# First half's attention by pairs of heads, block by block inside the second half's pairs

## The chip, the cores and the metric

The kernel runs on one core of one Trainium2 chip. The metric is the device time of one execution in microseconds (us); a run's time is compared as the median of several executions. The profile records one execution of its own. Its engines are PE (TensorE, matrix products; PEld is its weight load), DVE (VectorE), ACT (ScalarE), POOL (GpSimd) and SP (the queue that issues the DMAs).

## The reference

One layer of a streaming encoder: a norm with conditioning, one input projection, two groups of heads (an RWKV-7 recurrence and a forgetting attention, eight heads of 64 each), one output projection onto the concatenation of both, a gated residual, and a feed-forward part with a second gated residual. 1024 frames are a new stream, 64 are the next frames of another stream that has 256 cached frames. The change touches only the attention of the 1024 frames and what stands beside it:

```python
def _fox_attend(q, k, v, lc_q, lc_k, pos_q, pos_k):
    s = jnp.einsum('bqhd,bshd->bhqs', q, k, preferred_element_type=jnp.float32) * (HEAD_DIM ** -0.5)
    decay_bias = jnp.transpose(lc_q, (0, 2, 1))[..., :, None] - jnp.transpose(lc_k, (0, 2, 1))[..., None, :]
    causal = pos_k[None, :] <= pos_q[:, None]
    p = jax.nn.softmax(jnp.where(causal, s + decay_bias, -jnp.inf), axis=-1)
    return jnp.einsum('bhqs,bshd->bqhd', p.astype(v.dtype), v)
...
    mix = jnp.concatenate([y_rwkv, y_fox], axis=-1) @ w_out
    x = x + gt1[:, None] * mix
```

## The kernel before

**Halves.** The frames are worked in two halves, `Half(0)` with frames 0 to 511 and `Half(1)` with frames 512 to 1023 and the 64 frames of the other stream (576 columns). `phase` (from line 1595) runs the input projection and the recurrence for one half after the other, in an order written out by hand (`ORDER`). Keys and queries go to DRAM (`kx`, `qx`) in a high and a low part, since a float32 product is made of three products of parts; values go there by tokens (`vtok`), and for the first half also split into parts, by `put_v` (line 849), into `vscr`. What remains of the recurrence after the second half's projection (`late`, line 1758) is one head pair's norm.

**The first half's attention** (`attend`, line 927) goes head by head. Each head has two units of 256 queries. A unit makes the scores of its queries (two products and a causal mask each, line 956 to 962), takes the row maximum on VectorE, the exponential with the row sum on ScalarE, scales, transposes the result on the tensor engine, splits it into two parts, and multiplies both with the split values. `Pipe(2)` keeps two units in flight besides the one that is started. The heads' outputs go to DRAM (`yscr`). Heads 0 to 2 run while the recurrence's memory is still held, heads 3 to 7 after it. Beside heads 5 to 7 the operands and the row maxima of the second half's first pair are made (lines 1787 to 1791).

**The second half's attention** (`att_second`, line 1244) goes by pairs of heads, four of them. Operands come in by `pair_load` (line 1045) in three parts: 0 for the maxima, 1 for the scores, 2 for the values. `att_max` (line 1071) makes scores only to take row maxima; `att_rows` (line 1097) puts the negated maxima into a row of an operand, so that the scores come out shifted. `att_main` (line 1109) then makes the scores with the keys on the partitions, block by block of 128 keys, takes the exponential straight from PSUM, adds the blocks up for the denominators (`total`; VectorE for one head, GpSimd for the other), multiplies with the values, float32 without a split (`values`), and at the end makes the denominators with a product by ones. No transposition of the scores is needed. `att_main` stops ("h", "b", the block's number, "v") so that `att_second` can put other work between: the maxima of the next pair, and the output projection of the first half (`proj_steps`, line 1225), 64 steps of three products, as its operands arrive by `load_mix` (line 1284) from `yscr` and is split. In this stretch `te.on` is set: the tensor engine's instructions keep the order of the program. Elsewhere a scheduler orders each engine's instructions.

**Memory.** A pool of tiles that is opened where others were closed waits tile by tile until what lay there is no longer used. The second half's operands (`pair_ops`, line 1024) lie where the recurrence's tiles were. PSUM has eight banks; the second half's attention uses three for scores (`st`), two for maxima and small results (`mx`), two for the projection (`mm`), one for the values (`pv`).

**After it** come the second half's output projection (`outproj`), the feed-forward part (`ffn`) and its second product (`down`), which the change leaves as they are.

Of the kernel before, what the change touches and what calls it, by code (L numbers as in the profile page):

```python
# [64 lines left out]
class K:  # L65
# [782 lines left out]

    def put_v(self, j, src, b0, nb, rows):

        nc = self.nc
        s = src.rearrange("p i (h d) -> p i h d", h=2)
        for h in range(2):
            vs = self.slot([P, 4, 2, 64], F32R, name="vs", tag="fx")
            d = vs[0:rows, 0:nb]
            nc.vector.tensor_copy(d[:, :, 0], s[:, :, h])
            nc.vector.tensor_tensor(d[:, :, 1], s[:, :, h], d[:, :, 0].bitcast(F32), op=ALU.subtract)
            nc.sync.dma_start(self.vscr[2 * j + h][0:rows, b0:b0 + nb], d.rearrange("p i x d -> p i (x d)").bitcast(F32))
# [24 lines left out]
    def att_consts(self, ap):  # L883
# [11 lines left out]
        self.nmx = [ap.tile([P, 64], F32, name=f"nmx{x}") for x in range(2)]  # L895
# [3 lines left out]
    def att_pools(self, es, R):  # L899
        nc = self.nc  # L900
        self.tpool = MultiPool({t: R(es, "t" + t, b) for t, b in (("pth", 3), ("ptl", 3), ("nm", 4), ("ls", 4))})
        self.spool.pools.update({"fy": R(es, "sfy", 2), "avt": R(es, "savt", 2)})

    def att_ops(self, p, sets):

        return [[p.tile(s, F32R, name=f"{n}x{i}") for n, s in (("qs", [P, 512]), ("q2", [68, 512]), ("k1", [P, 512]),
                                                                  ("k2", [68, 512]), ("vs", [P, 4, P]))] for i in sets]

    def att_load(self, hd, hf):
        nc = self.nc  # L910
        qs, q2, k1, k2, vs = self.ops[hd > 1][hd % 2]
        n, t0 = hf.n, hf.t0
        NK = SP + PAST + SS if hf.smp else 512
        nc.sync.dma_start(qs[:, 0:n].bitcast(F32), self.qx[hd, 0:128, t0:t0 + n])
        for r in (0, 64):
            nc.sync.dma_start(k1[r:r + 64, 0:NK].bitcast(F32), self.kx[hd, 0:64, 0:NK])
        for r in (slice(0, 64), slice(64, 68)):
            s = slice(64 + r.start, 64 + r.stop)
            nc.sync.dma_start(q2[r, 0:n].bitcast(F32), self.qx[hd, s, t0:t0 + n])
            nc.sync.dma_start(k2[r, 0:NK].bitcast(F32), self.kx[hd, s, 0:NK])  # L920
        if hf.smp:
            nc.sync.dma_start(vs[:, 0:10].bitcast(F32), self.vscr[hd][:, 0:10])
            nc.sync.dma_start(vs[0:SS, 10].bitcast(F32), self.vscr[hd][0:SS, 10])
        else:
            nc.sync.dma_start(vs[:, 0:4].bitcast(F32), self.vscr[hd][:, 0:4])

    def attend(self, hd, hf):

        nc = self.nc
        j, h = hd // 2, hd % 2  # L930
        hs = slice(64 * h, 64 * h + 64)
        qs, q2, k1, k2, vs = self.ops[hd > 1][hd % 2]
        n, t0 = hf.n, hf.t0
        if hd > 1:
            self.att_load(hd, hf)
        if h == 0:
            self.fy = self.slot([P, n], name="fy", tag="fy")
        fy = self.fy
        qps = list(range(2, 5) if hf.smp else range(2))

        def unit(qp):
            smp = qp == 4
            nq = SS if smp else 256
            kb = 3 if smp else 2 * qp + 2
            pTs = []
            ptiles = []
            for t in range(1 if smp else 2):
                q0 = SP if smp else (2 * qp + t) * P
                nk = 320 if smp else q0 + P
                k0 = SP if smp else 0  # L950
                qn = SS if smp else P
                pq = self.ps([P, 1024 if hf.smp else 512], tag="sc", name="psc")
                c = 0
                while c < nk:
                    w = 320 if smp else min(512, -(-(nk - c) // 256) * 256)
                    nc.tensor.matmul(pq[:, c:c + w], qs[:, q0 - t0:q0 - t0 + P], k1[:, k0 + c:k0 + c + w], start=True,
                                     stop=False, skip_group_check=True)
                    nc.tensor.matmul(pq[:, c:c + w], q2[0:68, q0 - t0:q0 - t0 + P], k2[0:68, k0 + c:k0 + c + w], start=False,
                                     stop=False, skip_group_check=True)
                    c += w  # L960
                cm = 0 if smp else nk - qn
                nc.tensor.matmul(pq[0:qn, cm:cm + qn], self.identb[0:qn, 0:qn], self.cmask[0][0:qn, 0:qn], start=False,
                                 stop=True, skip_group_check=True)
                nm = self.tpool.tile([P, 1], F32, tag="nm", name="nm")
                ls = self.tpool.tile([P, 1], F32, tag="ls", name="ls")
                nc.vector.tensor_reduce(nm[0:qn], pq[0:qn, 0:nk], axis=AX.X, op=ALU.max, negate=True)
                p = self.tpool.tile([P, 1024 if hf.smp else 512], F32, tag="p", name="p")
                nc.scalar.activation(p[0:qn, 0:nk], pq[0:qn, 0:nk], AF.Exp, bias=nm[0:qn], accum_out=ls[0:qn])
                nc.vector.reciprocal(ls[0:qn], ls[0:qn])
                self.flip = (self.flip + 1) % 3  # L970
                if self.flip == 0:
                    nc.scalar.activation(p[0:qn, 0:nk], p[0:qn, 0:nk], AF.Copy, scale=ls[0:qn])
                else:
                    nc.vector.tensor_scalar(p[0:qn, 0:nk], p[0:qn, 0:nk], ls[0:qn], None, op0=ALU.mult)
                ptiles.append((p, qn, nk))
            yield 1
            for b0 in range(0, kb, 2):
                pt = self.ps([P, 2, 256], tag="tr", name="ppt")
                pT = [self.tpool.tile([P, 2, 256], F32R, tag=t, name=t) for t in ("pth", "ptl")]
                pTs.append(pT)  # L980
                for b in range(b0, min(kb, b0 + 2)):
# [10 lines left out]
                elif not smp and b0 + 2 == kb:  # L992
                    for t in pT:
                        nc.gpsimd.memset(t[:, 1, 0:P].bitcast(F32), 0.0)
# [249 lines left out]
    def att_second(self, hf, h0, g):  # L1244
# [6 lines left out]
        for j in range(4):  # L1251
# [26 lines left out]
            if j == 2:  # L1278
                mix = self.load_mix(hf)
# [769 lines left out]
```

## Time and profile before

| | us |
|---|---|
| median of three runs | 1715.62 |
| lowest and highest run | 1715.6 and 1720.08 |
| profiled execution | 1710.58 |
| its span, first to last instruction | 1708.9 |
| PE busy | 1634.3 (96%) |
| DVE busy | 1073.4 (63%) |
| ACT busy | 686.0 (40%) |
| POOL busy | 163.7 (10%) |

The page divides the span into 40 slices of 42.7 us and gives each engine's busy share in tenths. The tensor engine stands at 9 nearly everywhere and at 7 in the 17th and 18th slices, from 684 to 769 us, which is most of the first half's attention. The granted clock (PEclk) is at 5 in the 18th slice and at 8 in the 19th. A matrix product's duration contains its way through the array; products follow each other closer than that, so the price of one is read from start to start. A product at half clock counts as busy all the time it takes.

### The profile page before, as it was taken

The numbers are of one execution on the slowest core, as the hardware profiler recorded it, in microseconds if no ns is written. First come the engines' busy times: TensorE is split into PE (matmuls) and PEld (weight loads), VectorE is DVE, ScalarE is ACT, GpSimd is POOL, SyncE is SP. The second block draws the span as 40 slices with busy tenths as digits, with TensorE's granted clock in tenths as the row PEclk, the third lists the DMA queues.
The fourth block names the chain that finished last, engine by engine and source line by source line (L and its number), as shares of the span: only waits on it lengthen the run. The fifth ranks groups of instructions, "written<-read, shape, count | busy, mean of one in ns | idle before, by whom it ended". The sixth has DMA issues, their size and how long they took to land.

```text
span 1708.9 us, 32239 instructions
## 1 busy us (share of the span) xinstructions
PE 1634.3 (96%) x12811; PEld 1409.5 (82%) x12811; DVE 1073.4 (63%) x2264; ACT 686.0 (40%) x1374; POOL 163.7 (10%) x312
## 2 busy tenths in 40 slices
PE   5999999999999999779999999999999999999999
PEld 3667667788878887555668999999999999999998
DVE  6676675758866644756556995555555555555545
ACT  4544465654445445624335652322332233211210
POOL 1101101020201103202341000000000000000000
PEclk9999999999989999958999999999999999999999
DMA  8434376621233253645634423222222214433313
GB/s 315 154 109 138 105 211 193 191 70 50 54 90 89 77 147 116 195 130 146 170 125 144 165 100 104 82 80 79 81 80 80 77 64 158 148 100 96 96 38 124
DMA packets 131909, 203.81 MB, mean 119 GB/s; under 512 B 61966, under 2 KB 68654, under 8 KB 131758
## 3 DMA queue, kind: packets, MB, share of 16 engines
q1 hardware_dynamic: 131758, 201.75, 38.6%
q8 instruction: 101, 1.65, 0.4%
q14 instruction: 50, 0.41, 0.1%
HBM read 155.62 MB, written 46.07 MB: 118 GB/s over the span
## 4 chain that ended last, share of the span: by engine, by line
PE 49%; DMA 2%; DVE 1%; ACT 1%; SPq 1%; issue 1%; DVEq 0%
PE pd L1582 15%; PE pfe L1467 8%; PE pfc L1467 7%; PE pfa L1467 7%; PE pfb L1467 4%; PE po L1929 2%; PE pst L1929 2%; PE pav L1929 1%; DMA kax<-kx 1%; PE pmx L1929 1%; PE po L325 1%; PE po L323 1%; PE po L324 1%; SPq L1049 1%; DMA kbx<-kx 0%
## 5 line engine op out<-in xcount | busy, mean ns | idle before, releaser
L323 PE MATMUL pmm<-hhi,whi 128*128 128x288 f32 (+1 forms) x624 | 221.2, 355 | 4.0 <-ACT pb L346 4.0
L324 PE MATMUL pmm<-hlo,whi 128*128 128x288 f32 (+1 forms) x624 | 217.8, 349 | 0.9 <-DVE hlo L301 0.7
L325 PE MATMUL pmm<-hhi,wlo 128*128 128x288 f32 (+1 forms) x624 | 215.5, 345 | 0.0
L241 ACT CAST whi<-wraw 128x1024 fp32r<-128x1024 f32 (+2 forms) x116 | 99.3, 856 | 216.8 <-PE pd L1582 165.0
L1582 PE MATMUL pd<-al,whi 128*128 128x512 f32 (+1 forms) x528 | 172.4, 327 | 0.0
L1582 PE MATMUL pd<-ah,whi 128*128 128x512 f32 (+1 forms) x528 | 172.2, 326 | 0.0
L1582 PE MATMUL pd<-ah,wlo 128*128 128x512 f32 (+1 forms) x528 | 172.2, 326 | 0.0
L1586 DVE SCALAR_TENSOR_TENSOR x1t<-pd,mod,x1t 128x512 f32<-128x512 f32 x192 | 91.2, 498 | 109.1 <-PE pd L1582 108.5
L323 PEld LDWEIGHTS pmm<-hhi,whi 128*128 128x128 f32 x624 | 120.2, 193 | 19.3 <-ACT pb L346 5.8
L324 PEld LDWEIGHTS pmm<-hlo,whi 128*128 128x128 f32 x624 | 120.3, 193 | 12.8 <-issue 2.1
L325 PEld LDWEIGHTS pmm<-hhi,wlo 128*128 128x128 f32 x624 | 119.9, 192 | 11.6 <-issue 2.2
L245 DVE TENSOR_TENSOR wlo<-wraw,whi 128x1024 fp32r<-128x1024 f32 (+2 forms) x108 | 104.2, 965 | 31.0 <-ACT whi L241 30.6
L1582 PEld LDWEIGHTS pd<-ah,whi 128*128 128x128 f32 x528 | 99.0, 188 | 7.1
L1582 PEld LDWEIGHTS pd<-ah,wlo 128*128 128x128 f32 x528 | 99.1, 188 | 7.1
L1582 PEld LDWEIGHTS pd<-al,whi 128*128 128x128 f32 x528 | 99.1, 188 | 7.0
L1467 PE MATMUL pfc<-hh,hS 128*128 128x256 f32 (+1 forms) x352 | 101.8, 289 | 1.1 <-ACT hh L1369 1.1
L1467 PE MATMUL pfa<-hh,whi 128*128 128x256 f32 (+1 forms) x352 | 102.1, 290 | 0.0
L1467 PE MATMUL pfc<-hh,lS 128*128 128x256 f32 (+1 forms) x352 | 101.8, 289 | 0.0
L1467 PE MATMUL pfa<-hl,whi 128*128 128x256 f32 (+1 forms) x352 | 101.7, 289 | 0.0
L1467 PE MATMUL pfa<-hh,wlo 128*128 128x256 f32 (+1 forms) x352 | 101.5, 289 | 0.0
L1467 PE MATMUL pfc<-hl,hS 128*128 128x256 f32 (+1 forms) x352 | 100.7, 286 | 0.0
L1414 ACT CAST hS<-wraw 128x512 fp32r<-128x512 f32 x88 | 53.6, 619 | 62.7 <-PE pfc L1467 61.5
(421 smaller groups left out, 4160.2 us busy)
## 6 DMA issues: line engine op xcount, KB each, us to landing
wraw<-in_w_in_dram SPq DMA_DIRECT2D x52, 512.0 KB
wada<-in_w_ada_dram SPq DMA_DIRECT2D x48, 512.0 KB
as<-actscr SPq DMA_DIRECT2D x22, 544.0 KB
wraw<-in_w_gate_dram SPq DMA_DIRECT2D x22, 512.0 KB
wraw<-in_w_up_dram SPq DMA_DIRECT2D x22, 512.0 KB
wraw<-in_w_down_dram SPq DMA_DIRECT2D x40, 256.0 KB
wraw<-in_w_out_dram SPq DMA_DIRECT2D x16, 512.0 KB
actscr<-sg SPq DMA_DIRECT2D x22, 288.0 KB
```

Of the source, the lines that this page charges most:

```text
L241: nc.scalar.copy(hi, src)
L245: eng.tensor_tensor(lo, src, hi.bitcast(F32), op=ALU.subtract)
L323: nc.tensor.matmul(ps[0:M, 0:n], whi[:, k, 0:M], xhi[:, k, off:off + n], start=(k == 0), stop=False)
L324: nc.tensor.matmul(ps[0:M, 0:n], whi[:, k, 0:M], xlo[:, k, off:off + n], start=False, stop=False)
L325: nc.tensor.matmul(ps[0:M, 0:n], wlo[:, k, 0:M], xhi[:, k, off:off + n], start=False, stop=(k == kt - 1))
L1049: ld = lambda d, s: nc.sync.dma_start(d.bitcast(F32), s)
L1414: nc.scalar.copy(w[x][0], src)
L1467: nc.tensor.matmul(ps, l[:, k], r[:, s, k], start=(first and k == 0 and y == 0), stop=(k == 3 and y == 2), skip_group_check=True)
L1582: nc.tensor.matmul(ps[:, 0:n], w[:, i], x[:, t:t + n], start=(i == 0 and y == 0), stop=(i == len(fs) - 1 and y == 2))
L1586: nc.vector.scalar_tensor_tensor(dst, ps[:, so - off:so - off + l], self.mod[:, 40 + o, b:b + 1], dst, op0=ALU.mult, op1=ALU.add)
L1929: return self.pin(self.tc.nc.tensor.matmul(*a, **k))
```

## The change

The first half's attention goes by pairs as well. Pair 0 runs alone, beside the rest of the recurrence, with operands of its own (`pair_first`). Pairs 1 to 3 run inside the second half's pairs: `low_steps` makes a generator of 39 steps, and `att_second` takes one of them at each stop of the second half's own generator, 25 stops a pair, before any other filler. The operands of pairs 1 to 3 are tiles that lie idle then: the mixes of both halves (`mixhi`, `mixlo`), of which pair 3 takes over those of pair 1; their exponentials and sums lie in the tile of the residual (`x1`). So the residual's loads and the loads of the mixes start when pair 3 is done, and the output projection two blocks later, now three steps a block. Outputs of pairs 1 to 3 are split into the mixes at once; only pair 0's goes by `yscr`, and `load_mix` brings five parts in place of eight. `attend`, `att_load`, `att_ops`, `att_pools`, `put_v` and `Pipe` go. The PSUM pools of the attention are opened ahead of pair 0, and the tiles of `pair_ops` lie in another order. While `te.on` is set, `total` gives the second head's adds to GpSimd in either half. There are four tiles of maxima in place of two.

```diff
-        else:
-            self.put_v(j, vt, 0, 4, P)
...
+    def pair_first(self, pool):
+
+        g = {n: [pool.tile([r, 512], F32R, name=f"{n}f{h}") for h in range(2)]
+             for n, r in (("kb", 73), ("qc", 73), ("ka", P), ("qa", P), ("qb", 73))}
+        for h in range(2):
+            self.ones_keys(g["kb"][h])
+            self.no_rows(g["qc"][h])
+        return self.pair_bufs(g, True)
+
+    def pairs_low(self):
+
+        (m0, m1), (l0, l1) = self.mixhi, self.mixlo
+        a, b, c, d, e, f = [[t[:, k, 0:512] for k in range(4)] for t in (m0.a, l0.a, m1.a, l1.a, m0.b, l0.b)]
+        one = {"kb": a[0:2], "qc": a[2:4], "ka": b[0:2], "qa": b[2:4], "qb": c[0:2]}
+        two = {"kb": c[2:4], "qc": d[0:2], "ka": d[2:4], "qa": [e[2], f[2]], "qb": [e[3], f[3]]}
+        out = [None, one, two, dict(one)]
+        x, n = self.x1[0], [0]
+
+        def pt():
+            n[0] += 1
+            return x[:, n[0] % 6]
...
+            free = iter((6, 7))
+            g["pt"], g["acc"] = pt, lambda free=free: x[:, next(free)]
+            self.pair_bufs(g, False)
+        return out
...
-                eng = nc.gpsimd if h and hf.smp else nc.vector
+                eng = nc.gpsimd if h and te.on else nc.vector
...
-        if hf.smp:
+        if hf.smp or j:
             self.split(self.mixhi[hf.i][:, 4 + j, 0:n], self.mixlo[hf.i][:, 4 + j, 0:n], fy[:, 0:n])
...
+    def low_steps(self, hf, gs):
+
+        fill = lambda it, n: [next(it, None) for _ in range(n)]
+        for j in (1, 2, 3):
+            mx = self.att_max(j + 1, hf, gs[j + 1]) if j < 3 else iter(())
+            last = 0
+            for b in self.att_main(j, hf, gs[j]):
+                if b in ("h", "b"):
+                    fill(mx, 2 * (last > 1))
+                elif b == "v":
+                    if j == 1:
+                        for x in range(3):
+                            self.pair_load(3, hf, gs[3], x)
+                    fill(mx, 99)
+                    if j < 3:
+                        self.att_rows(j + 1, hf, gs[j + 1])
+                else:
+                    last = b + 1
+                yield
...
             for b in self.att_main(j, hf, g):
+                if low and next(low, 1) == 1:
+                    low, mix = None, self.load_mix(h0)
+                    fill(mix, 2)
+                    self.residual_x(h0)
+                    start = 8 * j + (b if isinstance(b, int) else 7) + 2
...
-                    fill(po, self.MIX[b])
+                    if start and 8 * j + b == start:
+                        po = self.proj_steps(h0)
+                    fill(po, 3)
                     fill(mx, b % 2)
-                if b == 2 and j == 0:
-                    self.residual_x(h0)
...
+            for _ in self.att_main(0, halves[0], self.g0):
+                pass
             at0.close()
             mid.close()
...
+            self.pair_load(1, halves[0], gs[1], 0)
+            for x in range(3):
+                self.pair_load(0, halves[1], g, x)
+                if x:
+                    self.pair_load(1, halves[0], gs[1], x)
+            for j, hf, q in ((1, halves[0], gs[1]), (0, halves[1], g)):
+                for _ in self.att_max(j, hf, q):
+                    pass
+                self.att_rows(j, hf, q)
...
+            self.att_second(halves[1], halves[0], g, self.low_steps(halves[0], gs))
```

More of the change, by code (lines that the diff above doesn't have):

```diff
@@ L1030, in pair_ops, with pair_bufs @@
         for t in self.pops["kb"]:
-            self.nc.gpsimd.tensor_copy(t[64:69], self.ones[64:69, 0:1].to_broadcast([5, nk]))
+            self.ones_keys(t)
         for t in self.pops["qc"]:
-            self.nc.gpsimd.memset(t[64:69].bitcast(F32), 0.0)
+            self.no_rows(t)
             self.nc.gpsimd.memset(t[:, 576:640].bitcast(F32), 0.0)
+    def pair_bufs(self, g, big):
+        for n, m in (("pt", 512), ("acc", 512), ("r", 512), ("fy", 576)):
+            if n not in g:
+                g[n] = lambda n=n, m=m: self.tpool.tile([P, m], F32, tag=n, name=n)
+        g["tags"] = {"st": "st", "mx": "mx", "pv": "pv" if big else "mm", "sm": "mx"}
+        return g
@@ L1064, in pair_load @@
                 ld(ka[:, 0:NK], self.kx[hd, 0:128, 0:NK])
-        if part == 2:
+        if part == 2 and not hf.smp:
+            g["v"] = self.tpool.tile([P, 4, P], F32, tag="v0", name="v0")
+            nc.sync.dma_start(g["v"], self.vtok[j][:, 0:4])
+        elif part == 2:
             v = g["v"]
@@ L1287, in load_mix @@
         mh, ml = self.mixhi[hf.i], self.mixlo[hf.i]
-        for m in range(4 if hf.smp else KT):
+        for m in range(4 if hf.smp else 5):
             t = self.slot(name="mixt", tag="fs")
@@ L1780, in run @@
+            p = L(mix1, "mix1")
+            high = [rows4(p, halves[1], x) for x in ("mixrh", "mixfh", "mixrl", "mixfl")]
             self.x1 = [L(x1s, "x1p0").tile([P, KT, 512], F32, name="x1_0")]
-            self.tpool.pools["pc"] = L(attp, "tpc", 2)
             self.pair_ops(L(attp, "attp"))
-            g = self.pair_get(0)
-            mx = self.att_max(0, halves[1], g | {"tags": {"mx": "ch"}})
-            for hd in range(3, 8):
-                pipe.run(self.attend(hd, halves[0]))
-                if hd > 4:
-                    self.pair_load(0, halves[1], g, hd - 5)
-                for _ in range(16 * (hd > 5)):
-                    with tc.issue_after(self.av.ins):
-                        next(mx, None)
@@ L1801, in run @@
-            self.mixlo = [Rows(rows4(p, hf, "mixrl"), rows4(p, hf, "mixfl")) for p, hf in zip(mps, halves)]
-            self.spool.pools.update({"fs": L(mix0, "sfs", 2)})
-            self.tpool.pools.update({t: R(att, "t" + t, b) for t, b in (("pt", 6), ("acc", 2), ("r", 1), ("fy", 1), ("pts", 1),
-                                                                        ("accs", 1))})
-            PB = lambda es, name, b: E(es, name, b, space=PSUM, reuse_waits="tile")
-            self.pspool = MultiPool({t: PB(att, "p" + t, b) for t, b in (("st", 3), ("pv", 1), ("mm", 2), ("mx", 2))})
```

233 lines of the change are left out of this document (51 added, 182 removed).

## The prediction

> **What bounds the kernel now.** I read the windows view first, because the change touches one stretch only: from the end of the projections (671 us) to the start of the second half's output projection. Its columns are the stretch, its length, the busy time of each engine, then the granted TensorE clock and the DMA share and rate.
>
> ```profile
> span 1708.9 us, 32239 instructions
> ...
> core 0: us, PE busy (x) PEld busy (x) DVE busy (x) ACT busy (x) POOL busy (x), PEclk, DMA share, GB/s
> 671.00:693.00 22.00, 16.81 (x103) 12.46 (x101) 18.08 (x49) 16.09 (x46) 5.26 (x15) 1.00 0.64 199
> 693.00:728.00 35.00, 25.55 (x137) 19.09 (x138) 24.49 (x72) 21.40 (x66) 8.68 (x24) 0.87 0.65 176
> 728.00:768.00 40.00, 31.60 (x103) 21.18 (x103) 24.16 (x58) 10.74 (x33) 1.17 (x6) 0.50 0.47 134
> 768.00:780.00 12.00, 11.09 (x34) 8.34 (x34) 5.34 (x11) 5.07 (x10) 0.72 (x1) 0.50 0.36 110
> ...
> 812.00:850.00 38.00, 36.03 (x183) 22.89 (x182) 20.66 (x36) 13.73 (x26) 14.45 (x11) 0.96 0.58 162
> ```
>
> The first half's eight heads run from 671 to 768; the second half's pairs from 768 on. In the first part no engine is full: from 693 to 768 the tensor engine is busy 57 of 75 us, and much of that only because its clock has fallen to 0.50 (103 products in 40 us, against 183 in 38 us later). From 780 on it is full at full clock. The waits view (693 to 768, then 768 to 912) says who holds it, and the chain of waits what follows:
>
> ```profile
> PE pav L1008 <- DVE fy L1015: 6.4, 5, 1.7
> ...
> PE pss L1929 <- DMA kax<-kx: 2.6, 3, 1.1
> ...
> 910.87 5.71 PE po L1929 x24
> ...
> 1445.30 260.03 PE pd L1582 x1584
> ```
>
> So each head is a chain of small steps through three engines (no single wait above 1.7 us, yet the clock falls). The second half's stretch ends with the last 24 products of the first half's output projection, at 916.6 us; behind it the chain is mostly tensor-engine work to the end. Whatever the stretch 671 to 916.6 loses or gains, the end loses or gains.
>
> **The change, part by part.** *Before the second half's pairs.* What is left of the recurrent heads ends here, with its store on the queue:
>
> ```profile
> 693.01 0.33 SPq L694 DMA_DIRECT2D yscr<-y  x1
> ```
>
> Pair 0 of the first half now runs beside that tail, in place of heads 0 to 2. Its maxima, scores and values are 9.6 us of tensor work (worked out below) and it has until 693 to finish; I count nothing for it, and up to 5 us if its chain (maxima, row of maxima, exponentials, denominators) outlasts the tail. Then the operands of two pairs must land, because the new loop's first products read both.
>
> ```profile
> kbx<-kx SPq DMA_DIRECT2D x4, 336.0 KB
> kax<-kx SPq DMA_DIRECT2D x2, 672.0 KB
> ...
> qcx<-qx SPq DMA_DIRECT2D x4, 144.0 KB
> ...
> 720.00:725.00 5.00, 3.46 (x23) 2.54 (x20) 2.96 (x11) 3.86 (x11) 0.76 (x4) 1.00 1.00 216
> 735.00:740.00 5.00, 4.23 (x14) 2.66 (x13) 3.35 (x9) 0.00 (x0) 0.00 (x0) 0.50 1.00 299
> ```
>
> Second half, pair 0: two kb of 336 KB, two ka of 672, eight query tiles of 144 (two qc, two qb, two qa written twice) are 3.17 MB by KB. First half, pair 1: ten pieces of 64x512 float32 (128 KB) and two ka of 256 KB, 1.8 MB. With the DMA engines full (share 1.00) the rows show 216 GB/s for a time of 2 KB rows and 299 for one of long rows: 11 us and 8.5 us, with the last landing about 21 us. Most of the second half's operands lie where the recurrent pools were, so they start at 693, and the loop starts at **714**. The maxima of both pairs run under these loads: twenty reductions of 0.28 to 0.69 us (VectorE rows below), about 10 us, for the second half's pair, and 4 for the other. The fast end is 705 (pair 1's operands lie in free space and may land before 693: 12 us); the slow end 726 (5 MB at the 176 GB/s of the row 693 to 728, and pair 0 late: 33 us).
>
> *Pairs 1 to 3, inside the loop.* They add tensor work to a stretch that is already full. The price of each kind, start to start in the timeline of the tensor engine (one line of the chain of waits last):
>
> ```profile
> 799.81 0.28 PE L1929 MATMUL pst<-qbx,kbx 73*128 73x256 f32 x1
> 799.93 0.23 PE L1929 MATMUL pst<-cmask,identb 128*128 128x128 bf16 x1
> 799.98 0.48 PE L1929 MATMUL po<-mixfh,whi 128*128 128x512 f32 x1
> 800.30 0.39 PE L1929 MATMUL po<-mixfl,whi 128*128 128x512 f32 x1
> 800.53 0.40 PE L1929 MATMUL po<-mixfh,wlo 128*128 128x512 f32 x1
> ...
> 802.23 0.87 PE L1929 MATMUL pav<-pt,vx 128*64 128x256 f32 x8
> 802.93 0.28 PE L1929 MATMUL pvs<-pTs,vx 128*64 128x64 f32 x4
> ...
> 807.39 1.08 PE L1929 MATMUL psm<-acc,ones 128*64 128x512 f32 x4 [0.45 <-DVE qbx L1105]
> 808.40 0.50 PE L1929 MATMUL po<-mixfh,whi 128*128 128x512 f32 x1
> ...
> 811.20 0.27 PE L1929 MATMUL pss<-qax,kax 128*128 128x64 f32 x1 [1.04 <-DMA kax<-kx]
> ...
> 796.45 1.65 PE pav L1929 x8
> ```
>
> 512 columns take 0.23 us, 256 take 0.12, 384 by proportion 0.17; a mask 0.05 and 0.09 more on the product behind it (0.32 for 0.23), so 0.14. One pair of the first half: maxima 2 x (0.12+0.12+0.17+0.23) + 8 masks = 2.40; scores twice that many products, 2.56 + 1.12 = 3.68; values 1.65 + 0.70 (its last two blocks have these widths); denominators 1.01; one transposition 0.14. Sum **9.6 us**, three pairs 28.7, less pair 1's maxima and transposition, which run before: **+26**. That is what the tensor engine does anyway in the old heads; what goes is only their waiting and the half clock.
>
> *The other terms of the loop.* The old one lasts 916.6 - 768 = 148.6. Its cold start (12 us at clock 0.50, 11.09 busy) costs 5.5 and goes, but the new one also starts after thin work; I take 5 for that, between 2.5 and 8. The order on the tensor engine is fixed there, so a waiting product holds both streams. At the border of the second half's pairs 0 and 1 the output projection no longer covers the loads:
>
> ```profile
> 799.15 0.45 SPq L1049 DMA_DIRECT2D qax<-qx  x1
> ```
>
> From this first issue to the product that waited (811.20) are 12 us, under which six projection steps of 3 x 0.23 lay: 4.2 us. Now one step of the first half's pairs (39 steps for 28.7 us, so 0.7) lies there: +3.5, and 2.5 for the clock behind it, **+6**. At the second border the projection runs again. At the end the projection is used up (64 steps: 12 in pair 1, 30 in pair 2, 22 in pair 3), so the last pair's denominators and split stand uncovered where 24 products (5.71 us) lay; the output projection's first products cover about half: **+3**. The residual's four loads (2 MB, 7 to 10 us at the rates above) move from before 693 to the end of pair 3; two blocks and eight steps cover them, and two PSUM buffers beyond that.
>
> *VectorE.* In pair 0 of the second half it now has to do its own and almost two other pairs:
>
> ```profile
> L1092 DVE TENSOR_REDUCE pc<-pmx 128x1 f32<-128x512 f32 x30 | 20.5, 687 | 8.3 <-PE pmx L1929 7.9
> L1149 DVE TENSOR_TENSOR acc<-acc,pt 128x512 f32<-128x512 f32 x12 | 13.5, 1126 | 2.2 <-ACT pt L1133 2.1
> ...
> L1147 DVE TENSOR_TENSOR acc<-pt 128x512 f32<-128x512 f32 x4 | 3.0, 748 | 1.9 <-ACT pt L1133 1.9
> ...
> L1092 DVE TENSOR_REDUCE pc<-pmx 128x1 f32<-128x128 f32 x6 | 1.7, 284 | 0.5 <-PE pmx L1929 0.3
> ...
> L1149 POOL TENSOR_TENSOR acc<-acc,pt 128x512 f32<-128x512 f32 x12 | 18.0, 1498 | 15.3 <-ACT pt L1133 15.3
> ```
>
> A first-half pair is 8 maxima between 284 and 687 ns (3.9 us) and by my estimate 3.4 of sums, rows and output: 7.3. One step goes with each of the second half's 25 steps a pair, and a first-half pair has 13, so 1.92 of them lie in pair 0 and the last ends after 1.6 pairs. With 20 for the second half's pair (the row 812 to 850) pair 0 has 20 + 1.92 x 7.3 = 34 us of VectorE against 44 of the tensor engine: 25 of its own (the row's 38 less 16 projection steps of 0.7 and 2 idle) and 1.92 x 9.6. Not the bound, but the two maximum buffers are shared by both streams: **+3**, between 0 and 8.
>
> *Elsewhere.* The value splits of the first half go, off any chain:
>
> ```profile
> L856 DVE CAST vs<-tok x8: 277/290/295, 124.6 to 315.9; 128x256 fp32r<-128x256 f32 x8
> ```
>
> Nobody waited for them; zero. Three mix loads and splits and three stores of the first half fall away too, under full tensor work: zero, bounded by a microsecond either way.
>
> **Sum.** 148.6 - 5.5 + 26 + 5 + 6 + 3 + 3 = 186; 714 + 186 = 900 against 916.6: **-17 us**. The profiled execution took 1710.6 us, 1.7 beyond its span, and lies 5.0 below the median 1715.6; I take the difference over to the median: 1715.6 - 17 = **1698.6**. Fast ends: 705 + (143 + 26 + 2.5) = 876.6, -40, 1676. Slow ends: 726 + 194 = 920, +3, 1719.
>
> **A rule against it.** One of the adds of every first-half pair moves to GpSimd. The rows show a 512-wide add at 1126 ns on VectorE beside GpSimd's 1498, and 748 for the form that starts the sum. The Trainium skill, "SBUF — State Buffer", section "Who interferes with whom", says that a VectorE instruction with two SBUF inputs and a GpSimd one that reads SBUF block each other entirely; by that the rows' slowdown would be expected, and the trace agrees (1126 for 748).
>
> **The rivals.** *(a) Adds block each other.* A first-half pair puts adds of 384, 256 and 128 columns on GpSimd, by 1498 ns per 512 columns 2.2 us; if VectorE stands still for all of it and is the bound, three pairs cost 6.6 more: 1705. For it: the 1126. Against: VectorE has 10 us to spare in pair 0.
>
> *(b) The loads get ahead.* Nothing holds pair 1's operands back and the queue is free once the old head loads are gone: start 705 and a cheap start, about 1680.
>
> *(c) The loads stay behind.* They queue behind pair 0's store and run at the average rate: start 726, end 912, 1711; no difference to be told.
>
> *(d) Slower: the half clock comes into the loop.* This decides between gain and loss:
>
> ```profile
> 700.00:704.00 4.00, 2.12 (x14) 1.74 (x14) 1.90 (x6) 0.91 (x3) 0.47 (x3) 1.00 0.71 209
> 704.00:708.00 4.00, 3.05 (x12) 1.84 (x11) 2.70 (x10) 2.13 (x8) 0.00 (x0) 0.64 0.69 179
> ...
> 712.00:716.00 4.00, 3.15 (x19) 2.02 (x18) 3.83 (x11) 3.47 (x13) 0.69 (x4) 1.00 0.02 8
> ...
> 724.00:728.00 4.00, 2.25 (x14) 2.06 (x13) 1.74 (x4) 1.49 (x4) 0.53 (x3) 0.70 0.73 169
> ```
>
> Behind four microseconds with the engine busy 2.1 to 2.3 the clock is lost; with 3.15 it is kept. Until the projection starts, nothing but two attention streams fills the fixed order: 26 + 1.6 x 25 = 66 us of work. If waits for maximum buffers thin it below 0.6, each microsecond at half clock costs one more: half the stretch is +33, 1732; the point of no gain is a quarter of it. For it: the old heads did just this. Against: two independent streams lie side by side, and 34 of VectorE stand against 44. The Trainium skill, "TensorE: Matmul & The Clock Gate", section "HAM oscillation — how this bites in real kernels", has gaps over about 3.4 us as what loses the clock. By that rule the stretch would stay fast; the trace does not agree, since the clock fell with no wait above 1.7 us.
>
> **How the numbers follow.** Forecast 0.50; (a) 0.10, (b) 0.14, (c) 0.12, (d) 0.14. A difference under 0.3% (5 us) can't be told from no change here. Faster is the forecast, (a) and (b): 0.74; same (c): 0.12; slower (d): 0.14. The range runs from the fast to the slow ends, 1676 to 1719, and leaves out (d) and little else.
>
> **What would show it.** First pss near 714 and the end of po and psm near 900 in the timeline; tensor clock back at 1.00 some 8 us after the start; 9 to 10 us per first-half pair; pss waiting 4 to 6 us on kax once, in pair 1; VectorE under 40 us in pair 0's stretch. Wrong if the start lies past 730, or if windows of the loop's first half show the tensor engine under 0.6 busy or at 0.50.

## The result, and the profile after

| | before | after |
|---|---|---|
| median of 20 runs each, us | 1714.6 (1707.3 to 1720.1) | 1705.4 (1694.2 to 1715.9) |
| ratio, 95% interval | | 0.9948 (0.9929 to 0.9967) |
| profiled execution, us (span) | 1710.6 (1708.9) | 1703.8 (1702.1) |

The changed kernel is about 9 us faster, just over half of the 17 that were forecast, and inside the range. One slow run among all that are reported here, 1805.3 us at a mean granted clock of 0.83 in the kernel "splits, no stores" below, is left out of its row. The page of the profiled execution (the row is the granted tensor clock in 40 slices, in tenths):

```profile
span 1702.1 us, 31944 instructions
...
PEclk8999999999999999587999999999999999999999
```

Around the change the clock is low for three slices (5, 8, 7), where the kernel before had two (5, 8). To see where the time went I cut the attention at its two ends: the tail's last store yscr<-y, and the first product of the second half's output projection. Windows view of the kernel before, from its store at 693.0 to the second half's pairs, and on to the end; columns as in the prediction, so idle time is the length less PE busy, and time lost to the clock the length times one less PEclk:

```profile
693.00:768.00 75.00, 57.14 (x238) 40.27 (x239) 48.65 (x130) 32.15 (x99) 9.84 (x30) 0.67 0.55 154
768.00:916.41 148.41, 142.33 (x703) 91.60 (x702) 82.20 (x136) 61.04 (x115) 52.26 (x38) 0.94 0.51 152
```

The same for the changed kernel: from its store at 679.1 to the first product of the loop (the first cache score pss, at 706.5; in the kernel before it stands at 767.5), from there to the dense part of the loop, and on to the end. The last row is the dense part as far as the border of the second half's pairs 0 and 1:

```profile
679.06:706.47 27.41, 18.68 (x57) 10.30 (x53) 15.99 (x31) 1.23 (x2) 5.99 (x8) 0.56 0.84 222
706.47:719.50 13.03, 5.60 (x20) 4.30 (x19) 2.21 (x4) 1.69 (x3) 0.29 (x1) 0.50 0.74 185
719.50:908.57 189.07, 181.34 (x850) 113.61 (x850) 95.06 (x158) 68.76 (x132) 63.68 (x54) 0.86 0.44 127
719.50:773.00 53.50, 49.55 (x231) 29.30 (x231) 27.61 (x55) 16.46 (x35) 14.07 (x17) 0.79 0.41 109
```

The stretch took 223.4 us and takes 229.5: it is not shorter but 6 longer. Idle time is the same (17.9 + 6.1 = 24.0 before, 16.2 ahead of the dense part + 7.7 in it = 23.9 after); time lost to the clock went from 24.8 + 8.9 = 34 us to 18.6 + 26.5 = 45. The old heads' waits became a wait for operands, and their half clock moved into the loop. The end still comes 7.8 us earlier, because the store comes 14 earlier, at 679.1 for 693.0: a gain ahead of the store, in the projections, which the forecast had at nothing. How much of the 14 is chance of these two executions comes below.

Timeline of the changed kernel's tensor engine where the loop begins:

```profile
706.47 0.39 PE L1860 MATMUL pss<-qa,ka 128*128 128x64 f32 x1
...
710.53 0.79 PE L1860 MATMUL pst<-qa,ka 128*128 128x512 f32 x1
...
712.41 0.33 PE L1860 MATMUL pst<-cmask,identb 128*128 128x128 bf16 x1
719.54 0.76 PE L1860 MATMUL pmx<-kb,qc 73*128 73x512 f32 x1 [6.80 <-DMA mixrh<-qx]
```

The cache scores and the first score block run, and then the engine stands for 6.80 us (7.96 in a second profile) at the first maximum of the second half's pair 1. It reads kb and qc, whose loads are issued from 713.5 on, behind thirteen loads for the first half's pair 2 (nine of queries, four of keys, from 703.7 on). The line names another load, which landed then; that it is the kb and qc is put to the test by the swap below. Windows of the same kernel from there on:

```profile
715.00:720.00 5.00, 0.46 (x1) 0.49 (x2) 0.00 (x0) 0.00 (x0) 0.00 (x0) 0.50 0.96 223
720.00:725.00 5.00, 5.00 (x15) 3.49 (x15) 1.69 (x4) 2.28 (x4) 0.29 (x1) 0.50 0.96 208
730.00:735.00 5.00, 5.00 (x16) 2.78 (x18) 3.28 (x7) 0.94 (x2) 1.95 (x2) 0.50 0.01 3
735.00:740.00 5.00, 5.00 (x24) 2.05 (x20) 0.13 (x1) 0.41 (x1) 0.00 (x0) 0.80 0.00 0
770.00:775.00 5.00, 4.16 (x18) 3.08 (x18) 0.92 (x2) 2.38 (x5) 0.19 (x1) 0.61 1.00 242
780.00:785.00 5.00, 5.00 (x14) 2.16 (x13) 1.35 (x3) 2.22 (x5) 0.29 (x1) 0.50 0.00 0
795.00:800.00 5.00, 5.00 (x26) 2.26 (x22) 1.57 (x3) 1.39 (x3) 0.73 (x1) 1.00 0.00 0
```

From 719.5 the engine is busy without a gap, and yet for 17 us it works at half speed (15 and 16 products in 5 us); at the border of the pairs the same comes once more, for 22 us.

### The profile page after: what moved, and what is told of

Its sections match the earlier page's. It is cut to its first block, busy times and chain, and to the rows that moved or that the text cites. A ratio compares the mean times of both kernels' runs of the same rounds, so it can differ in the third digit from the quotient of the medians.

```text
span 1702.1 us, 31944 instructions
## 1 busy us (share of the span) xinstructions
PE 1635.9 (96%) x12783; PEld 1400.2 (82%) x12783; DVE 1050.2 (62%) x2162; ACT 660.6 (39%) x1284; POOL 180.0 (11%) x314
## 4 chain that ended last, share of the span: by engine, by line
PE 78%; DVE 8%; ACT 4%; DMA 4%; issue 2%; SPq 2%; POOL 0%; DVEq 0%; ACTq 0%; POOLq 0%
PE pd L1515 15%; PE pfe L1400 8%; PE pfc L1400 8%; PE pfa L1400 7%; PE pmm L323 4%; PE pmm L325 4%; PE pmm L324 4%; PE pfb L1400 4%; PE pst L1860 3%; PE pbs L404 2%; PE po L1860 2%; PE pav L1860 2%; PE pmx L1860 1%; PE pS L662 1%; SPq L958 1%
```

## The experiments

One thing holds for all: the time of one kernel varies by some 20 us from run to run, and much of that is the clock. Each run lists its span and its mean granted clock; span times one less clock is the time lost to the clock, and what remains moves less (for the changed kernel the deviation of the span is 5.5 us and that of the remainder 2.0; for the kernel before 3.8 and 3.1):

| kernel (runs) | median, us | ratio (95%) | mean span | of it lost to the clock | remainder (its deviation) |
|---|---|---|---|---|---|
| before (23) | 1715.6 | | 1713.0 | 56.0 | 1657.0 (3.1) |
| changed (20) | 1705.4 | 0.9948 (0.9929 to 0.9967) | 1703.6 | 49.7 | 1653.9 (2.0) |
| changed, again (12) | 1703.3 | 0.9942 (0.9920 to 0.9964) | 1703.7 | 49.4 | 1654.3 (1.6) |
| splits back (12) | 1712.3 | 0.9985 (0.9962 to 1.0008) | 1710.0 | 56.6 | 1653.4 (1.6) |
| splits, no stores (11) | 1716.9 | 1.0005 (0.9977 to 1.0033) | 1715.8 | 59.1 | 1656.7 (1.9) |
| loads swapped (6) | 1702.2 | 0.9929 (0.9903 to 0.9954) | 1700.6 | 47.3 | 1653.2 (2.4) |
| + idle products in loads (6) | 1697.3 | 0.9901 (0.9872 to 0.9929) | 1695.8 | 30.0 | 1665.8 (2.7) |
| + idle products in loop (6) | 1691.5 | 0.9852 (0.9827 to 0.9876) | 1689.3 | 18.3 | 1671.0 (2.0) |
| idle products in loop alone (6) | 1689.9 | 0.9866 (0.9835 to 0.9896) | 1689.4 | 29.6 | 1659.9 (1.0) |
| half as many (6) | 1697.8 | 0.9893 (0.9861 to 0.9925) | 1694.0 | 26.0 | 1668.1 (1.3) |
| serial pairs (10) | 1709.5 | 0.9957 (0.9932 to 0.9981) | 1706.6 | 47.8 | 1658.8 (2.3) |
| serial, idle products (12) | 1710.0 | 0.9967 (0.9947 to 0.9987) | 1707.5 | 16.8 | 1690.7 (1.7) |
| before, idle products (12) | 1714.4 | 1.0001 (0.9977 to 1.0025) | 1712.1 | 22.6 | 1689.6 (2.5) |

The "before" of each ratio ran beside it. Where idle products are added the remainder rises, because they take time themselves and because waits that stood at lower clock now stand at full clock; only the span counts there.

**Both kernels once more.** No edit.

> The changed kernel once more, beside the others of this call. Every theory expects what it gave before: 0.993 to 0.997 of the kernel before (about -9 us), the tail's store yscr<-y near 679 us, the tensor engine idle some 7 us near 712 to 720 for the next pair's query tiles, and the clock at 0.50 from about 680 to 737 and again near 773 to 795. If any of these moves by more than 3 us between two runs of one kernel, differences of that size between the variants say nothing.

> The kernel before once more, for a second profile of it: every theory expects its attention stretch (last store yscr<-y to the first product of the second half's output projection) at 223 us within 5, and the projections ahead of it to move by several us with the clock's stretches at 0.50, which lie elsewhere in each execution. If the stretch itself moves by 10 us between two profiles, the split of the gain between projections and attention from single profiles says nothing.

The changed kernel gave 0.9942. Its second profile has the store at 686.3 and a stretch of 226.7 us; the second of the kernel before has 699.3 and 228.9. So the stretch is good to some 5 us from one profile, the store to 7, and both arrangements take the same stretch within that: 223 and 229 against 229 and 227. For the projections, single profiles are not enough, hence the next two runs.

**The splits put back.** My theory was that the 14 us were either what the first half's value splits had cost or chance. The edit; a second kernel leaves out its last line, the store:

```diff
         if hf.smp:
             nc.sync.dma_start(self.vtok[j][0:SS, 8], vs)
+        else:
+            self.put_v(j, vt, 0, 4, P)
...
+            nc.vector.tensor_copy(d[:, :, 0], s[:, :, h])
+            nc.vector.tensor_tensor(d[:, :, 1], s[:, :, h], d[:, :, 0].bitcast(F32), op=ALU.subtract)
+            nc.sync.dma_start(self.vscr[2 * j + h][0:rows, b0:b0 + nb], d.rearrange("p i x d -> p i (x d)").bitcast(F32))
```

> The changed kernel with the value splits of the first half put back: eight times a cast, a subtraction and a store that nobody reads now. Theory U (removing the splits bought the 14 us upstream of the attention): the store yscr<-y of the tail moves from 679 back to 690 to 695, and the ratio to the kernel before rises from 0.995 to 1.000 to 1.003. Theory O (the upstream gain is the planner's other order of the projections, or a chance of scheduling): the store stays at 677 to 683 and the ratio at 0.995. My prediction priced these splits at zero, so by it the ratio would not move (within 0.001).

> The changed kernel with the value splits of the first half put back on VectorE, but without their stores; nobody reads them. With splits and stores the ratio was 0.9985 beside 0.9942 without, all of the difference in time at a lower clock (mean 57 against 49 us per execution) and none in the rest. Theory V (the 16 VectorE instructions make the projections thinner and that loses clock): ratio 0.997 to 1.000. Theory S (it is the stores on the queue): 0.993 to 0.996. Rival Z (chance between two builds: the difference isn't tied to either): anything between.

With the splits the gain is gone: 0.9985 and 1.0005. The first interval just touches that of the changed kernel, the second doesn't. The stores are not needed for it; the sixteen VectorE instructions are enough. Nearly all of the difference is time lost to the clock (56.6 and 59.1 us against 49.4), and the remainder moves by -1 and +2. The tail's store agrees: it stands at 689.6 to 707.4 (mean 696.6) in the five profiles of kernels with the splits, and at 679.1 to 694.4 (mean 687.0) in the nine without. So of the 14 us between the first two profiles about 10 go with the splits, and the rest is chance. Where the time is lost shows in the windows from 200 to 400 us, first the kernel without stores (its profile is the slowest of its eleven runs, 1732.3 us), then the changed one:

```profile
200.00:400.00 200.00, 194.07 (x1616) 150.43 (x1614) 128.35 (x312) 107.61 (x216) 26.21 (x56) 0.93 0.47 137
```

```profile
200.00:400.00 200.00, 195.84 (x1721) 153.66 (x1720) 140.77 (x345) 111.18 (x225) 28.30 (x60) 1.00 0.48 139
```

In this stretch all five profiles with the splits (two kernels before, both of these, and the last of the table) have the clock at 0.93 to 0.98; of the nine without, eight have 1.00 and one 0.98. No wait for the splits is behind it: others waited 0.8 and 0.4 us for them in all. The planner orders the tensor engine's products in this phase itself, and with the splits among its VectorE work it comes to another order. Timeline of the kernel before:

```profile
276.18 0.38 PE L575 MATMUL pvt<-ident,z 128*128 128x128 f32 x2
276.49 0.66 PE L588 MATMUL pw<-g,inv 32*32 32x32 f32 x15
...
277.61 0.62 PE L193 MATMUL pada<-wada,ct 128*32 128x128 f32 x10
278.16 0.69 PE L588 MATMUL pgt<-gt,At 32*32 32x32 f32 x16
...
280.82 0.69 PE L588 MATMUL pw<-g,inv 32*32 32x32 f32 x16 [0.25 <-DVE g L595]
281.44 0.50 PE L323 MATMUL pmm<-hhi,whi 128*128 128x512 f32 x1
```

For 5.3 us there are only small products (32x32 above all), and behind them the clock falls (0.57 from 281.5 to 285.5). In the five profiles with splits such a run of 4.2 to 5.6 us stands near 275, and in four of them the clock falls at its end (in the fifth at 270, behind another run of 3.9 us); in the nine without, the run there has 2.6 to 2.8 us. That the order does it, and not something else that comes with it, is argued from this alone.

**The two loads swapped.**

```diff
+            self.pair_load(1, halves[1], self.pair_get(1), 0)
             for x in range(2):
                 self.pair_load(2, halves[0], gs[2], x)
-            self.pair_load(1, halves[1], self.pair_get(1), 0)
```

> The changed kernel with two loads swapped on the queue: the query and key tiles of the second half's pair 1 of the first half's stream go ahead of the second pair's; everything on the other engines keeps its order. Theory Q (the 6.8 us idle at 712 to 719.5 are only the place in the queue): the idle time falls to under 2 us, the loop starts dense at about 713, and the end of the loop comes 5 to 7 us earlier (ratio about 0.991). Rival B (bandwidth: the same bytes must land first, whatever their order): the wait goes over to another operand of the same stretch, and the ratio stays within 0.994 to 0.996.

The loads that move ahead are kb and qc of the second half's pair 1. The 6.80 us wait is gone and no other of its size came for it, so the place in the queue was its cause. From store to first score block and on to the end it reads:

```profile
689.20:720.65 31.45, 22.20 (x71) 13.33 (x67) 17.63 (x33) 1.23 (x2) 6.01 (x8) 0.55 0.86 216
720.65:901.35 180.70, 173.42 (x857) 109.12 (x856) 97.96 (x160) 69.71 (x135) 64.76 (x55) 0.92 0.47 142
```

The time fell by only 1 to 3 us, which the intervals do not separate from nothing; this profile is the quickest of the six runs. The 20 us from there on still run at half clock (0.51).

**Idle products while the operands land.**

```diff
+    def warm(self, n):
+        ps = self.ps([P, 512], tag="mm", name="pwarm")
+        for _ in range(n):
+            self.te.matmul(ps[:, 0:P], self.ones, self.ident, start=True, stop=True, skip_group_check=True)
...
+            self.te.on = True
+            self.warm(12)
             for j, hf, q in ((1, halves[0], gs[1]), (0, halves[1], g)):
                 for _ in self.att_max(j, hf, q):
-                    pass
+                    self.warm(2)
+                self.warm(4)
                 self.att_rows(j, hf, q)
```

> The kernel of e2 with some 40 idle float32 products on the tensor engine while the loop's operands land (results read by nobody), so that the engine isn't thin between the tail of the recurrence and the loop. Theory C (the half clock carried into the loop costs it 8 to 9 us in its first 17 us of dense work): the clock stands at 1.00 when the loop starts, the first 17 us of products shrink to 9, and the time falls by 6 to 9 us under e2's. Rival N (the loop's first stretch is held by operands and VectorE, not by the clock): the clock is at 1.00 and the end of the loop moves by less than 2 us. Rival W (the products themselves delay the maxima of the first pairs): slower than e2.

The time is 5 us lower than with the swap alone, at the edge of what can be told. The clock did stay at 1.00 through the loads, and was then lost at the loop's own start. Windows and timeline:

```profile
715.00:720.00 5.00, 4.13 (x31) 3.75 (x31) 2.21 (x5) 0.49 (x1) 0.00 (x0) 1.00 1.00 250
720.00:725.00 5.00, 3.96 (x13) 2.67 (x12) 1.47 (x4) 2.34 (x4) 0.29 (x1) 0.63 0.65 176
```

```profile
719.24 0.21 PE L1869 MATMUL pss<-cmask,identb 64*64 64x64 bf16 x1
...
721.70 0.76 PE L1869 MATMUL pmx<-kb,qc 73*128 73x512 f32 x1 [1.04 <-DMA kb<-kx]
```

What stands there are twelve cache scores pss of 64 columns with two masks (2.9 us, with a wait of 0.87 us behind the first), one score block, and a wait of 1.04 us. So the theory went on: not the loads, but this thin place, and its like at the border.

**Idle products in the loop's thin places, with and without those in the loads.** To the edit above, or to the swap alone, three places are added:

```diff
                         self.att_rows(j + 1, hf, nxt)
+                        if low:
+                            self.warm(16)
...
             fill(po, 1)
+            if low:
+                self.warm(8)
...
+            if j < 2:
+                self.warm(8)
             pt = self.tpool.tile([P, 2, 3, SS], F32, tag="pts", name="pTs")
```

> The kernel with idle products during the loads, with more of them at three further places (results read by nobody): 8 behind the cache scores pss of the second half's pairs 0 and 1, 16 behind the row of maxima at the end of pair 0, and 8 ahead of pair 1. In the run with products during the loads alone the clock stood at 1.00 until the pss of pair 0, was lost there (about 722) and came back only at 741, and was lost again from 773 to 782: some 10 and 4 us of half clock. Theory C (thin places of the fixed order start each half-clock stretch, and dense float32 products there prevent it): both stretches go, the end of the loop comes 8 to 13 us earlier than in that run, ratio to the kernel before 0.982 to 0.986. Rival L (the clock falls in the loop whatever is put there, for instance because it follows the past load or chance): the stretches shift but stay, ratio 0.989 to 0.992. Rival W (the added products, 40 at 0.10 us, cost their 4 us on a full engine): 0.992 or above.

> The run with idle products everywhere (0.985), without those during the loads: only the ones behind pss, behind the row of maxima and ahead of pair 1 stay. So the engine comes to the loop at half clock as in the changed kernel. Theory D (a dense run of float32 products brings the clock back where it stands): half clock until some 3 us behind the 8 products after pss, and 0.984 to 0.988, since the loads' stretch is bound by the DMA. Rival H (the loop's mixed products keep the clock down for another 15 us or more, as at 720 to 737, and 8 products are too short to change that): 0.989 to 0.993.

Both give some 24 us (0.9852 and 0.9866) and beat both kernels clearly; theory C and theory D held. The three places in the loop earn 11 to 12 us on top of the swap (0.9866 against 0.9929, intervals apart). What the idle products in the loads add to them can't be told from nothing: from the store to the first pss it takes 26.7 us with them at a clock of 1.00 and 27.2 without them at 0.56, so the clock does not set the time there. Windows of the kernel with these alone, from store to first score block and on to the end, and the timeline of the place behind pss:

```profile
683.20:717.54 34.34, 25.31 (x86) 16.45 (x83) 18.20 (x35) 1.72 (x3) 5.97 (x8) 0.55 0.83 215
717.54:892.25 174.71, 168.76 (x923) 109.48 (x921) 97.86 (x158) 68.63 (x134) 64.71 (x55) 0.99 0.48 144
```

```profile
714.22 0.26 PE L1872 MATMUL pss<-cmask,identb 64*64 64x64 bf16 x1
714.41 3.37 PE L1872 MATMUL pwarm<-ident,ones 128*128 128x128 f32 x16
717.54 0.47 PE L1872 MATMUL pst<-qa,ka 128*128 128x512 f32 x1
```

The loop comes in at half clock here too; eight idle products (sixteen records, 3.1 us at half speed) bring it to 1.00 at 717.2, and from there the loop takes 174.7 us at 0.99. The changed kernel took 198.0 from its first score block (710.53) to the end, and the profile with the swap alone 180.7. That profile lost less to the clock at the border than the others, so single profiles do not divide the gain between swap and idle products; the medians do.

**Half as many.** 8, 4 and 4 in the loop, and half at the start and the ends of the maxima in the loads.

> The run with idle products everywhere, with half as many at each place of the loop (8, 4 and 4 in place of 16, 8 and 8) and half as many at the start and the end of the maxima. Theory T (half is enough to hold the clock; the other half stood on a full engine at 0.2 us each): 1.5 to 4 us less, ratio 0.983 to 0.9845. Rival K (too few: the clock is lost at pss or at the border): 0.987 to 0.990.

It gave 0.9893, and rival K came: the clock was lost behind pss. A wait stands there that the run with twice as many did not have. Timeline:

```profile
725.23 0.23 PE L1875 MATMUL pst<-cmask,identb 128*128 128x128 bf16 x1
727.89 0.47 PE L1875 MATMUL pmx<-kb,qc 73*128 73x512 f32 x1 [2.42 <-DMA kb<-kx]
```

The engine comes to the next pair's kb earlier, waits 2.42 us for it, and goes on for 17 us at half clock. That the eight products had also kept the engine busy until that load was in is my reading: with them the maximum that reads it starts without a wait.

**Pairs one after another.** Pairs 1 to 3 run to their end ahead of the loop. A second kernel adds two idle products a step and those of the 0.985 run.

```diff
-            self.att_second(halves[1], halves[0], g, self.low_steps(halves[0], gs))
+            low = self.low_steps(halves[0], gs)
+            for _ in low:
+                pass
+            self.att_second(halves[1], halves[0], g, low)
```

> The changed kernel with pairs 1 to 3 of the first half run to their end, one after another, before the second half's loop, in place of block by block inside it: the same operations, not interleaved. Theory I (the interleaving hides the small waits of these pairs): three pairs alone take 15 to 20 us each against 9.6 of tensor work, much of it at half clock, and the loop gets only 29 us shorter: ratio 1.003 to 1.02. Rival P (the tensor work counts, not its place): within 0.993 to 0.998 as the changed kernel.

> Pairs 1 to 3 one after another ahead of the loop, as in the serial run (0.9957), with idle products in all thin places (two a step in the pairs, and those of the 0.985 run). Theory I (with the clock held, the interleaving does hide the pairs' waits): three pairs take some 13 us each against 9.6 of tensor work, ratio 0.990 to 0.995. Rival P (interleaved or not makes no difference here either): 0.984 to 0.988.

Without idle products the serial form is as fast as the interleaved one within the intervals (0.9957, 0.9942): theory I falls, rival P holds. The serial form has no wait of 6.80 us for kb and qc, so the kernel with the loads swapped is the nearer comparison (0.9929); those intervals overlap too. Windows: loads, the three pairs alone, then the loop.

```profile
685.90:717.15 31.25, 21.20 (x64) 11.85 (x61) 18.92 (x37) 1.23 (x2) 6.02 (x8) 0.55 0.77 203
717.15:760.71 43.56, 38.54 (x160) 20.18 (x160) 19.25 (x39) 14.36 (x32) 4.84 (x8) 0.73 0.46 121
760.71:914.85 154.14, 142.40 (x705) 92.33 (x704) 82.42 (x127) 55.88 (x103) 53.09 (x38) 0.92 0.48 139
```

A pair alone takes 14.5 us, as theory I had it or a little less; what it missed is that the loop gets 35 us shorter without the pairs, and not 29, since they bring half clock along (26.5 us lost to the clock in the changed kernel's loop, 154.1 x 0.08 = 12.3 in this one). With idle products the result (0.9967) lies above both ranges and does not tell the theories apart: by the row below, from the loads' end, the pairs and the loop's start (713 to 800), the added products fill the tensor engine itself.

```profile
L1878 PE MATMUL pwarm<-ident,ones 128*128 128x128 f32 x236 | 36.0, 289 | 1.1 <-DVE fy L1132 1.0
```

**Idle products in the kernel before**, four ahead of every group of score, transpose and value products from head 3 on; one of the three places:

```diff
             pv = self.ps([P, 256], tag="av", name="pav")
+            self.warm(pv)
```

> The kernel before, with four idle products (results read by nobody) ahead of each head's scores, transposes and values from head 3 on, so that its eight-head stretch (693 to 768) doesn't thin out. Theory A (held at full clock, the old heads still wait for their chain of small steps, so the pairs' arrangement earns on its own): the clock stays up, the stretch loses at most 12 us, ratio 0.993 to 0.998, clearly above the 0.985 that the changed kernel gave with idle products. Rival B (the clock is all there is to win here, and the arrangement adds nothing): 0.984 to 0.989. Rival W (some 180 products at 0.2 us stand in the chain): 0.999 or above.

1.0001. The old heads' stretch ran at full clock:

```profile
689.60:768.75 79.15, 76.88 (x628) 70.93 (x628) 49.41 (x131) 33.31 (x98) 9.74 (x30) 1.00 0.54 153
```

But it is no shorter (79.2 us, where it had 75.0), for the engine is now busy 76.9 of 79.2 us, more than half of it with added products (392 records in the rows below, 0.11 us from start to start).

```profile
L931 PE MATMUL psc<-ident,ones 128*128 128x128 f32 x160 | 22.0, 279 | 0.0
L931 PE MATMUL ppt<-ident,ones 128*128 128x128 f32 x136 | 19.2, 280 | 0.0
L931 PE MATMUL pav<-ident,ones 128*128 128x128 f32 x96 | 13.4, 278 | 1.5 <-DVE fy L1024 1.5
```

This is rival W, and it leaves open what a leaner filling of the old heads would give, and with it how much of the 24 us needs the pairs' arrangement.

## Why the prediction was right in sign, and where it was wrong

| step | forecast | profiled execution after | second profile |
|---|---|---|---|
| tail's last store | 693.0 (projections at zero) | 679.1 | 686.3 |
| store to the first pss | 21 us | 27.4 | 27.2 |
| first pss to the end of the stretch | 186 us | 202.1 | 199.4 |
| end of the stretch | 900 | 908.6 | 913.0 |

The loop is cut here as the forecast cut it, from the first pss (714 forecast, 706.5 measured). The end moved by -7.8 us. Against the forecast of -16.6: -14.0 in the projections, +6.4 in the loads, +16.1 in the loop, which gives -8.1. So the sign was right by luck. All that the forecast lived on, the stretch behind the store, gave nothing (6 us longer), and the gain came from a term that was set to zero.

*"Elsewhere: zero" failed.* "Nobody waited for them" is true, and yet the splits cost 7 us (0.9985 against 0.9942) to 10, lost to the clock in the projections; that the order of the products does it was argued above and not shown. They are the whole gain that can be measured: with the splits back the change shows no difference.

*The loop (186) failed, by the clock.* The waits of its tensor engine, from 719 to 909 (total, times, longest):

```profile
PE pmx L1860 <- DMA mixrh<-qx: 6.8, 1, 6.8
PE psm L1860 <- DVE qb L1017: 2.7, 3, 1.8
PE pss L1860 <- DMA ka<-kx: 1.6, 2, 1.2
PE pss L1860 <- ACT r L1128: 0.7, 1, 0.7
PE pmx L1860 <- DVE nmx L1004: 0.6, 2, 0.3
...
PE pmx L1860 <- DVE pc L1004: 0.4, 2, 0.3
```

I split the loop of 202.1 us into work at full clock, idle time and what the clock costs while the engine is busy. In the dense part these are 154.8 (181.34 - 26.5), 7.73 and 26.5 us; ahead of it, at 0.50 all through, 2.8, 7.43 and 2.8. The old loop has 133.4 (142.33 - 8.9), 6.1 and 8.9.

Work: the three pairs add 157.6 - 133.4 = 24 us where I had 26. Idle: 15.2 us where the old loop's 6.1 and my 3.5, 3 and 3 came to 15.6. That is luck: 6.8 of it is the wait for kb and qc of the next pair, which I had no term for, since I had not looked up their place on the queue. For the maximum buffers I had 3 us and they cost 1.0 (0.6 and 0.4). VectorE is busy 27.6 us in the 53.5 of pair 0 (forecast 34) and never holds the tensor engine for more than 1.8. The border shows two short waits (1.8 us for qb ahead of psm, 0.7 ahead of pss), and not one of 4 to 6 on kax.

Clock: 29.3 us lost, of which up to 11 were in my sum (5 and 2.5, and 3.4 that the old loop had behind its cold start). The mis-sized term is this "cold start": I let the clock come back after 8 us as in the row 768 to 780. From the first pss it took 30 us, 17 of them in the dense part, and at the border 22 more.

*The loads (21 us) came to 27.4, inside their bounds of 12 to 33.* The row's rate times its length is 6.1 MB, where I had counted 5.0 (I left out the values, for one). At a clock of 1.00 the same stretch still takes 26.7 us, as said above, so the half clock in it is not what makes it longer.

*The signs.* My sign of a start past 730 did not come. The other one did: windows of the loop's first half stood at 0.50 (720 to 735), so by my own signs the account of the loop was wrong.

*Rival (d)* is what happened in the loop: in its dense part it lost 11 us to the clock up to the border (0.21 of 53.5) and 11 more behind it (22 us at half), past my point of no gain (a quarter of 66 us, 16.5), and the stretch was indeed no win. I had its cause wrong. It was to come from waits for maximum buffers; the runs with idle products put it to the cache scores with the wait behind them, and to the border. My argument against it, two streams that fill each other's gaps, is true of busy time and not of the clock. One of the rows that the forecast read for this rival, 724 to 728, also says less than I took from it: with 0.70 over its 4 us the clock went some 1.6 us into the row, behind four microseconds with the engine busy 2.75 (720 to 724), and not behind 2.25.

*The rule that I weighed.* I set "HAM oscillation — how this bites in real kernels" in the Trainium skill's page "TensorE: Matmul & The Clock Gate" (gaps over some 3.4 us) against the trace. The later traces disagree as well: the clock was lost where the longest gaps were 1.04 and 2.42 us. The same page of the Trainium skill, section "What's actually happening", has it come back after one busy window of about 3.4 us. With idle products (2.8 us) the trace agrees; in the loop of the changed kernel (17 us busy without a gap) it does not.

The adds on GpSimd, rival (a), decided nothing, since the tensor engine never waited more than 1.8 us for VectorE in the loop.

## What to carry to other kernels

When two streams are merged to fill a tensor engine, look at the granted clock and not only at its busy share: thin places (products of few columns, a wait of a microsecond at the start or at a border) were followed by 17 to 22 us of half speed each here, and some forty idle products behind such places, 0.2 us each, took 11 us off, where the merging itself earned nothing that could be measured. List what the first products of a fixed order read, and follow each operand back to its place on the queue. Instructions that nobody waits for are not free where a planner orders the rest: take them out alone and measure.

## What the runs showed of the hardware

The clock falls with the tensor engine busy too: in the kernel before it did so right behind 5.3 us of products of 32x32 and 128 columns, 5.25 of 5.5 us busy and with no wait above 0.25 us. It does not come back in every busy stretch: in the changed kernel 17 us of scores and maxima (256 to 512 columns, most with 73 rows, masks between) stayed at 0.50. In the kernel with idle products in the loop alone it was back 2.8 us behind the start of 3.1 us of dense 128x128 products. In the seven profiles where the loop's first scores ran at half clock it came back only within the first value products (128 rows, 512 columns, no masks between), 2.5 to 5.6 us behind their start: 3.0 in the changed kernel, 3.3 with the loads swapped, 5.6 with idle products in the loads. What it is about the scores and maxima that keeps the clock down wasn't settled. And the spread of one kernel's times is to a good part clock: over the changed kernel's 20 runs the deviation of the span is 5.5 us, and without the time lost to the clock 2.0; over 23 runs of the kernel before it is 3.8 and 3.1.

Adds of VectorE and GpSimd that overlapped went one behind the other, as the timeline of the kernel before shows for 512 columns: a VectorE add that started 0.04 us after one of GpSimd (at 783.4) took 1.78 us, where one alone took 0.68, and a GpSimd add that started 0.03 us after one of VectorE (at 787.7) took 1.80, where others took 1.27.
